# Two-layer trunk on one core: who multiplies the result's blocks by the last norm's weights

## The chip, the core and the metric

The kernel runs on one core of a Trainium2 chip. Its engines, as the profile names them: PE (TensorE, matrix products), DVE (VectorE), ACT (ScalarE), POOL (GpSimd) and SP (SyncE, which here only issues transfers). Each works through its own instructions in the order in which they stand in the program, and waits on semaphores for the others. The metric is the device time of one execution in microseconds; the median of several runs counts.

## The reference

With a depth of 1 the trunk has one layer, the attention, between two norms. The sequence has 256 rows, the model 4096 columns, 32 heads of 128:

```python
def rms_norm(x, g):
    xf = x.astype(jnp.float32)
    y = xf * lax.rsqrt(jnp.mean(xf * xf, axis=-1, keepdims=True) + RMS_EPS)
    return (y * g.astype(jnp.float32)).astype(x.dtype)

def attn_branch(xn, w_in, w_out):
    proj = xn @ w_in                               # 4096 x 16384
    q, k, v, g = jnp.split(proj, 4, axis=-1)
...
    o = stick_breaking_attention(to_heads(q), to_heads(k), to_heads(v))
...
    return (o * jax.nn.silu(g)) @ w_out            # 4096 x 4096

def reference(x, norm_attn, w_in_attn, w_out_attn, ..., final_norm):
    h = x + attn_branch(rms_norm(x, norm_attn), w_in_attn, w_out_attn)
    return rms_norm(h, final_norm)
```

All is float32. The change concerns the last line: `h` is divided by the root of its rows' mean square and multiplied by `final_norm`, one weight per column.

## The kernel before

**Units.** The two weight matrices are worked through in 20 units: 16 of `w_in` (the projections), then 4 of `w_out` (1024 columns of the result each, as two blocks `c` and `c + 1` of 512 columns, each for two halves `t` of the 256 rows). A unit has 16 steps `s` of 256 rows of the weights. In a "mixed" unit a step multiplies 2 x 2 blocks by a scheme with seven products instead of eight (a few steps use all eight); the combined weights of such a step are sums of blocks.

**What each engine does with a step.** SP loads the weights' tiles (`raw`). For a step with seven products GpSimd's queue issues two more transfers (`add_block`) that add a second weight block onto a `raw` tile in place; VectorE forms the other sums in `raw` (`sums`, three instructions). Each float32 operand is split into a high half (`wh`, by ScalarE's cast) and a low half (`wl`, by VectorE's subtraction `wl<-raw,wh`), and a product is three matmuls: high by high, high by low, low by high. TensorE adds them up in PSUM (`acc`). There are seven buffers for `raw`, seven for `wh`, five for `wl`, and four of a small ring "gh", which holds rows such as `xres` and `grow` below.

**The order.** No order is written out by hand. The class `Plan` (lines 113 to 245) simulates the engines while the program is written: each piece of work has an engine, an assumed cost in ns and a key (when it is due), and each engine takes the waiting piece with the smallest key when it becomes free. The order found in this way is the order in the program. `vector_ns(512)` is 600.

**The result's blocks.** When a `w_out` unit is done, `combine` builds the four blocks `h` of 128 x 512 from PSUM. During the next unit, at due places spread over its steps, `blocks_out` and `block_out` (lines 1052 to 1076) do the following for each of the four: load the weights of the norm for the block (`grow`, the same 512 values for all rows), load the rows of `x` (`xres`), add them to `h` on VectorE, take the squares' sum on ScalarE (`sq`), and then multiply `h` by `grow` in place (`gain_on`, line 1047), due 8 us behind the addition. This holds for six of the eight blocks, that is for 12 multiplications, four in each of the last three units. The last two blocks get their weights at the very end together with the rows' factor (`rows_out`). The other six are only scaled by that factor then, on VectorE or ScalarE, and stored.

**What the multiplication waits for and who waits for it.** It waits for `grow`, for the addition and for the square, which reads `h`. The buffer of `grow` is given back to the ring "gh" after the second of a block's two multiplications, and the next `grow` or `xres` load, on SP's queue, may be the one that gets it. In the attention's part `p<-spill` loads on GpSimd's queue use the same ring. The norm's final scaling of a block in `rows_out` reads what the multiplication wrote.

**GpSimd's work.** Apart from a few constants at the start it only issues transfers: `add_block`'s pairs, and the stores and loads of the attention's result (`spill`, `p`).

Of the kernel before, what the change touches and what calls it, by code (L numbers as in the profile page):

```python
# [14 lines left out]
ALU = mybir.AluOpType  # L15
# [13 lines left out]
W = 2 * CW  # L29
# [71 lines left out]
def vector_ns(n):  # L101
    return 67 + 1.0417 * n
# [146 lines left out]
def kernel(  # L249
# [10 lines left out]
    nc = Plan(tc)  # L260
# [65 lines left out]
    def soon(c=4.0):  # L326
        return nc.here + 1e3 * c


    def dve(emit, n, key=None, more=0, **kw):  # L330
        n = n if isinstance(n, tuple) else (n,)
        cost = sum(vector_ns(m) for m in n) + 122 * (len(n) - 1) + more
        return nc.work("vector", cost, emit, soon() if key is None else key, **kw)
# [280 lines left out]
    for k in range(WARM):  # L614
# [12 lines left out]
        out=tri_f, in_=tri_f, compare_op=ALU.is_ge, fill=0.0, base=0, pattern=[[-1, P]], channel_multiplier=1,  # L627
# [4 lines left out]
        out=off_f, in_=off_f, compare_op=ALU.is_ge, fill=0.0, base=0,  # L632
# [351 lines left out]
    hs, xres, grow = {}, {}, {}  # L984
# [62 lines left out]
    def gain_on(c, t, key=None):  # L1047
        h = hs[c, t]
        yield nc.until(("grow", c))
        yield dve(lambda: nc.vector.tensor_tensor(out=h, in0=h, in1=grow[c], op=ALU.mult), W, key)  # L1050

    def block_out(c, t, key):

        h = hs[c, t]
        yield nc.take("gh")
        yield load_out(c, t)
        yield nc.until(("xres", c, t))
        yield nc.take("att")
        yield dve(lambda: nc.vector.tensor_tensor(out=h, in0=h, in1=xres[c, t], op=ALU.add), W, key)
        nc.give("gh")  # L1060
        yield from squares(c, t, c, ALL, key)
        nc.give("att")
        yield from gain_on(c, t, key + GAIN_LATER * 1e3)
# [270 lines left out]
```

## Time and profile before

| what | value |
|---|---|
| median of 3 runs | 1699.45 us (1698.41 to 1699.9) |
| the profiled execution | 1698.9 us |
| its span, from the first to the last instruction | 1697.1 us |
| mean granted TensorE clock | 0.997 |
| instructions | 25128 |
| the multiplications `h<-h,grow` on VectorE | 12, from 1461.8 to 1669.9 us |

The page of a profile gives busy times by engine and, from the last instruction backwards, the chain of work that ended last. An instruction stands as engine, operation, written tile <- read tiles, shape; nearly all have line 132, that of a helper through which the engines are called, so they are told apart by their tiles. In the views of instructions in order of time, the first two numbers are the start and the duration in us (merged instructions have a count x2, x3), and a bracket at the end gives the engine's idle time just before and what ended it. In the groups of waits, the numbers are the total in us, how often, and the longest.

### The profile page before, as it was taken

The page shows a single profiled execution, that of the slowest core. Times are in us where ns is not written, and L with a number is a line of the kernel's source. Part 1 is how long each engine was busy: PE and PEld are TensorE (multiplying, and loading weights), DVE is VectorE, ACT ScalarE, POOL GpSimd, SP SyncE. Part 2 cuts the span into 40 slices and gives each one's busy share as a digit, 9 for nine tenths or more (in the row PEclk, how much of TensorE's full clock was granted, in tenths as well). Part 3 has the DMA queues.
Part 4 walks back from the last instruction along what each step waited for, and adds up shares of the span by engine and source line. Part 5 has one row for each costly group of instructions (what it writes and reads, how often), then busy time and mean ns, then how long its engine had stood idle before and what let it go on. Part 6 is the DMA issues. An engine that isn't in the chain of part 4 may idle for free.

```text
span 1697.1 us, 25128 instructions
## 1 busy us (share of the span) xinstructions
PE 1680.2 (99%) x7776; PEld 1417.4 (84%) x7776; DVE 1602.0 (94%) x2025; ACT 1206.7 (71%) x1665; POOL 324.9 (19%) x400
## 2 busy tenths in 40 slices
PE   9999999999999999999999999999999999999997
PEld 7888888888888888888888888888888888888885
DVE  8899999999999999999999999999999978999997
ACT  8986767676767676767676767676868775656654
POOL 0012222121222222222212121212122111212110
PEclk9999999999999999999999999999999999999998
DMA  9978888878787878797978797979797978888895
GB/s 343 332 197 247 232 247 222 252 217 253 215 256 212 256 212 266 199 272 196 276 201 269 198 268 196 272 198 269 204 264 210 300 230 266 245 245 256 246 304 185
DMA packets 248438, 412.77 MB, mean 243 GB/s; under 512 B 28016, under 2 KB 72560, under 8 KB 248304
## 3 DMA queue, kind: packets, MB, share of 16 engines
q1 hardware_dynamic: 194544, 354.24, 62.7%
q0 software_dynamic: 53472, 56.65, 20.0%
q8 instruction: 61, 1.00, 0.2%
q14 instruction: 73, 0.60, 0.1%
q10 hardware_dynamic: 288, 0.28, 0.1%
HBM read 402.93 MB, written 8.13 MB: 242 GB/s over the span
## 4 chain that ended last, share of the span: by engine, by line
PE 94%; DVE 3%; DMA 1%; issue 1%; ACT 1%; SPq 0%; DVEq 0%; ACTq 0%
PE acc L132 89%; PE z L132 3%; PE o L132 1%; DVE wl L132 1%; PE tr L132 1%; DVE h L132 1%; DVE raw L132 0%; ACT wh L132 0%; DMA raw<-in_w_out_dram 0%; DMA raw<-in_w_in_dram 0%; DMA xres<-in_x_dram 0%; SPq L132 0%; ACT sq L132 0%; DVE scalars L132 0%; DVE qk_sb L132 0%
## 5 line engine op out<-in xcount | busy, mean ns | idle before, releaser
L132 ACT CAST wh<-raw 128x1024 fp32r<-128x1024 f32 (+1 forms) x989 | 919.3, 970 | 385.5 <-DVE raw L132 160.9
L132 DVE TENSOR_TENSOR wl<-raw,wh 128x1024 fp32r<-128x1024 f32 (+1 forms) x815 | 975.7, 1220 | 49.3 <-ACT wh L132 23.9
L132 PE MATMUL acc<-wh,sh 128*128 128x512 f32 x2048 | 771.9, 389 | 0.1
L132 PE MATMUL acc<-wh,sl 128*128 128x512 f32 x1898 | 727.1, 383 | 1.8 <-DVE sl L132 1.8
L132 PE MATMUL acc<-wl,sh 128*128 128x512 f32 x1748 | 668.9, 383 | 0.1
L132 PEld LDWEIGHTS acc<-wh,sh 128*128 128x128 f32 x2048 | 384.0, 188 | 77.9 <-DVE qk_sb L132 4.9
L132 POOL DMA_DIRECT2D raw<-in_w_in_dram x300 | 258.3, 947 | 972.2 <-DMA raw<-in_w_in_dram 375.1
L132 PEld LDWEIGHTS acc<-wh,sl 128*128 128x128 f32 x1898 | 356.0, 188 | 66.3 <-DVE sl L132 2.4
L132 PEld LDWEIGHTS acc<-wl,sh 128*128 128x128 f32 x1748 | 328.4, 188 | 55.6 <-DVE wl L132 0.4
L132 DVE TENSOR_TENSOR raw<-raw,raw 128x512 f32<-128x512 f32 x348 | 238.3, 688 | 15.3 <-DMA raw<-in_w_in_dram 11.7
L132 PE MATMUL acc<-wh,oh 128*128 128x512 f32 x512 | 192.4, 383 | 0.0
L132 PE MATMUL acc<-wh,ol 128*128 128x512 f32 x488 | 186.7, 383 | 0.0
L132 PE MATMUL acc<-wl,oh 128*128 128x512 f32 x464 | 177.6, 383 | 1.4 <-DVE wl L132 1.4
L132 DVE TENSOR_TENSOR wh<-raw,wh 128x512 fp32r<-128x512 f32 x174 | 119.7, 688 | 3.3 <-ACT wh L132 2.7
L132 DVE TENSOR_TENSOR raw<-raw 128x512 f32<-128x512 f32 x174 | 119.4, 686 | 0.0
L132 PEld LDWEIGHTS acc<-wh,oh 128*128 128x128 f32 x512 | 96.1, 188 | 17.3
L132 PEld LDWEIGHTS acc<-wh,ol 128*128 128x128 f32 x488 | 91.5, 188 | 16.1
L132 PEld LDWEIGHTS acc<-wl,oh 128*128 128x128 f32 x464 | 87.1, 188 | 17.6 <-DVE wl L132 2.2
L132 POOL DMA_DIRECT2D raw<-in_w_out_dram x48 | 41.5, 984 | 173.8 <-DMA raw<-in_w_out_dram 85.2
L132 ACT ACTIVATE f<-f 128x384 f32<-128x384 f32 x96 | 50.5, 526 | 3.0
L132 POOL DMA_DIRECT2D p<-spill x27 | 17.0, 676 | 89.9 <-DVE ol L132 32.0
L132 DVE SCALAR_TENSOR_TENSOR gv_sb<-acc,scalars,gv_sb 128x512 f32<-128x512 f32 x45 | 33.5, 745 | 0.0
(86 smaller groups left out, 765.7 us busy)
## 6 DMA issues: line engine op xcount, KB each, us to landing
raw<-in_w_in_dram SPq DMA_DIRECT2D x1024, 256.0 KB, 4.5
raw<-in_w_out_dram SPq DMA_DIRECT2D x256, 256.0 KB, 4.5
raw<-in_w_in_dram POOLq DMA_DIRECT2D x300, 128.0 KB, 5.2
p<-spill POOLq DMA_DIRECT2D x27, 256.0 KB, 4.6
raw<-in_w_out_dram POOLq DMA_DIRECT2D x48, 128.0 KB, 5.4
xr<-in_x_dram SPq DMA_DIRECT2D x16, 256.0 KB, 5.3
xres<-in_x_dram SPq DMA_DIRECT2D x16, 256.0 KB, 5.5
out_dram<-h SPq DMA_DIRECT2D x16, 256.0 KB, 2.8
```

The costliest lines, as they stand in the source:

```text
L132: return self.tc.keep_in_program_order(getattr(self.engine, name)(*args, **kw))
```

## The change

The multiplication by the last norm's weights goes from VectorE's instruction stream to GpSimd's. The instruction and its operands stay the same; it stands in GpSimd's queue among the transfers that this engine issues. The planner's assumed cost is 1000 ns instead of VectorE's 600. The due time is unchanged.

```diff
     def gain_on(c, t, key=None):
         h = hs[c, t]
         yield nc.until(("grow", c))
-        yield dve(lambda: nc.vector.tensor_tensor(out=h, in0=h, in1=grow[c], op=ALU.mult), W, key)
+        yield nc.work(
+            "gpsimd", 1000, lambda: nc.gpsimd.tensor_tensor(out=h, in0=h, in1=grow[c], op=ALU.mult), key
+        )
 
     def block_out(c, t, key):
```

## The prediction

> **What bounds the kernel now.** I read the page's busy line and chain first, then the stages of the last three units, then the waits of TensorE, and last the order of instructions on VectorE around the multiplications.
>
> ```profile
> PE 1680.2 (99%) x7776; PEld 1417.4 (84%) x7776; DVE 1602.0 (94%) x2025; ACT 1206.7 (71%) x1665; POOL 324.9 (19%) x400
> PE 94%; DVE 3%; DMA 1%; issue 1%; ACT 1%; SPq 0%; DVEq 0%; ACTq 0%
> ```
>
> TensorE is never idle for long: 94% of the chain is its own work, and VectorE, at 94% busy, is the only other engine with a real share. So work taken off VectorE is worth only what TensorE waits for it. The stages from 1450 us on, which hold all twelve multiplications (the first at 1461.8, the last at 1669.9 us, both shown below), say how much that is; the columns are from:to, length, then busy time and instructions of each engine.
>
> ```profile
> core 0: us, PE busy (x) PEld busy (x) DVE busy (x) ACT busy (x) POOL busy (x), PEclk, DMA share, GB/s
> 1450.00:1500.00 50.00, 50.00 (x229) 42.55 (x228) 47.89 (x56) 32.74 (x41) 12.04 (x14) 1.00 0.94 280
> 1500.00:1550.00 50.00, 49.71 (x225) 41.78 (x224) 47.74 (x57) 28.91 (x34) 8.71 (x11) 1.00 0.84 247
> 1550.00:1600.00 50.00, 48.92 (x223) 41.35 (x222) 48.52 (x58) 32.05 (x43) 9.77 (x12) 1.00 0.88 259
> 1600.00:1650.00 50.00, 50.00 (x227) 42.22 (x226) 47.21 (x61) 29.73 (x39) 8.36 (x11) 1.00 0.92 285
> 1650.00:1680.00 30.00, 30.00 (x138) 25.54 (x137) 26.53 (x33) 16.64 (x23) 0.86 (x1) 1.00 0.54 164
> ```
>
> ```profile
> PE acc L132 <- DVE wl L132: 1.4, 2, 1.1
> 1515.60 0.50 PE L132 MATMUL acc<-wl,oh 128*128 128x512 f32 x1 [0.29 <-DVE wl L132]
> 1581.34 0.49 PE L132 MATMUL acc<-wl,oh 128*128 128x512 f32 x1 [1.08 <-DVE wl L132]
> ```
>
> In these 230 us TensorE waits twice, 1.4 us together, both times for a low half (wl) from VectorE: once at the end of the first of the three units, once near the end of the second, never in the third. VectorE is at its limit just ahead of both. That is all that a lighter VectorE could win, and it is also where a heavier VectorE is paid for at once.
>
> **The change part by part.** Removed: twelve multiplications on VectorE.
>
> ```profile
> L132 DVE TENSOR_TENSOR h<-h,grow 128x512 f32<-128x512 f32 x12 | 8.3, 688 | 0.0
> 1577.11 0.70 DVE L132 TENSOR_TENSOR raw<-raw,raw 128x512 f32<-128x512 f32 x1
> 1577.71 0.70 DVE L132 TENSOR_TENSOR h<-h,grow 128x512 f32<-128x512 f32 x1
> 1578.32 0.70 DVE L132 TENSOR_TENSOR raw<-raw 128x512 f32<-128x512 f32 x1
> ```
>
> One takes 0.69 us, but the next starts 0.60 us after it (1577.71 to 1578.32), the last 0.09 us being overlapped. So 12 x 0.60 = 7.2 us of VectorE's time go, four per unit.
>
> Added: the same twelve on GpSimd, which does no arithmetic there now. The only rows of its arithmetic are at the start:
>
> ```profile
> 0.31 0.10 POOL L1321 MEMSET const-float32-0.0<- 128x1 f32 x1 [0.31 <-issue]
> 4.56 0.20 POOL L132 MEMSET squares_f<- 128x128 f32 x1 [3.19 <-DVE idle L132]
> 4.83 0.29 POOL L132 TENSOR_SCALAR_AFFINE_SELECT squares_f<-squares_f 128x128 f32<-128x128 f32 x1
> 5.34 0.40 POOL L132 TENSOR_SCALAR_AFFINE_SELECT squares_f<-squares_f 128x128 f32<-128x128 f32 x1
> 5.24 0.35 DVE L132 TENSOR_SCALAR sh<-xs,gcol 128x256 fp32r<-128x256 f32 x1 [0.71 <-DMA xs<-in_xT_dram]
> 6.63 0.34 DVE L132 TENSOR_SCALAR sh<-xs,gcol 128x256 fp32r<-128x256 f32 x1
> ```
>
> A fixed 0.10 us; 128 columns written take 0.20, read and written 0.29, and the same instruction takes 0.40 where VectorE reads SBUF beside it (5.24 to 5.59). These rows are the one hint in this trace that the two engines disturb each other. Scaled to 512 columns: 0.5 us by the memset (0.10 + 4 x 0.10), 0.86 by the quiet select, 0.10 + 4 x 0.30 = 1.30 by the disturbed one, 2.5 if the second operand doubles the disturbed rate. I take 1.30, since VectorE is nearly always at work in these units.
>
> What it costs VectorE isn't shown. One end: nothing, and VectorE simply gains 0.60 each time. The other: VectorE stands still for the whole of each multiplication, because nearly everything it does there (wl<-raw,wh; raw<-raw,raw; h<-h,xres) reads two operands in SBUF, as GpSimd's new instruction does. I take the second, being nearest to the disturbed row. VectorE's work then finishes before GpSimd's begins, so the 0.09 us of overlap is lost as well: 1.30 + 0.09 - 0.60 = 0.79, or 0.8 us more per multiplication.
>
> The Trainium skill, "SBUF — State Buffer", section "SBUF: two separate sides", speaks against the change in the same way: VectorE and GpSimd share a pair of ports, given as an exclusive lock for a whole instruction to a VectorE instruction with two SBUF inputs or to a GpSimd instruction that reads SBUF, and the loser blocks fully. Its "GPSIMD Engine Reference", section "Elementwise — side-by-side cycle accounting", measures 4497 ns for 2048 columns of such an addition; a quarter, 1.12 us as an estimate, would make the 0.8 us 0.6. Only the run can show either.
>
> Now place by place, with VectorE's order and its idle time ahead of an instruction in brackets:
>
> ```profile
> 1461.78 0.68 DVE L132 TENSOR_TENSOR h<-h,grow 128x512 f32<-128x512 f32 x1
> 1469.36 1.23 DVE L132 TENSOR_TENSOR wl<-raw,wh 128x1024 fp32r<-128x1024 f32 x1 [0.35 <-issue]
> 1482.61 1.23 DVE L132 TENSOR_TENSOR wl<-raw,wh 128x1024 fp32r<-128x1024 f32 x1 [0.26 <-PE acc L132]
> 1519.68 0.69 DVE L132 TENSOR_TENSOR wh<-raw,wh 128x512 fp32r<-128x512 f32 x1 [1.26 <-ACT wh L132]
> 1543.12 0.68 DVE L132 TENSOR_TENSOR h<-h,grow 128x512 f32<-128x512 f32 x1
> 1556.67 3.50 DVE L132 TENSOR_TENSOR wl<-raw,wh 128x1024 fp32r<-128x1024 f32 x3 [0.63 <-ACT wh L132]
> 1519.03 0.62 ACT L132 CAST wh<-raw 128x512 fp32r<-128x512 f32 x1 [3.17 <-DMA raw<-in_w_out_dram]
> ```
>
> First unit: from its first multiplication at 1461.8 to TensorE's wait at 1515.6 VectorE is idle 0.35 + 0.26 = 0.61 us. Four times 0.8 is 3.2, less 0.61: TensorE waits 2.6 us more. Second unit: from 1543.1 to 1581.3 it is idle 0.63 us, so 3.2 - 0.63 = 2.6 more. Between the two VectorE can catch up some of the first delay in the 1.26 us at 1519.7, which a weight transfer ended and not TensorE: less 1.3. Third unit: TensorE never waits, and VectorE is idle 50.00 - 47.21 + 30.00 - 26.53 = 6.3 us, which covers 3.2; without that cover it would be 3.2. Sum: 2.6 + 2.6 - 1.3 = 3.9 us. At the ends: hold of 0.5 us, nothing; hold of 2.5 us, 2.0 more per multiplication, 8.0 - 0.6 + 8.0 - 0.6 - 1.3 = 13.5, and 8.0 - 6.3 = 1.7 of the third unit, 15 us.
>
> GpSimd's queue is the other place. It issues the adding transfers (raw, twice per quad), and each multiplication now stands between them, waiting for ScalarE's square and for the weights of the norm.
>
> ```profile
> raw<-in_w_out_dram POOLq DMA_DIRECT2D x48, 128.0 KB, 5.4
> 1573.08 1.73 POOL L132 DMA_DIRECT2D raw<-in_w_out_dram  x2 [6.69 <-DVE raw L132]
> 1585.20 1.43 DVE L132 TENSOR_TENSOR raw<-raw,raw 128x512 f32<-128x512 f32 x2
> ```
>
> The pair at 1573.1 lands by about 1573.1 + 0.9 + 5.4 = 1579.4 and is first used at 1585.2, 5.8 us later. A multiplication of 1.3 us ahead of it is hidden by that; a longer one, above 5.8 us, would not be. I cost it at nothing. The last norm's output is hidden too: the final scaling comes 12 us behind the last multiplication, and its extra wait, now for another engine, is long over.
>
> ```profile
> 1669.90 0.69 DVE L132 TENSOR_TENSOR h<-h,grow 128x512 f32<-128x512 f32 x1
> 1682.41 0.49 DVE L132 TENSOR_SCALAR h<-h,scalars 128x512 f32<-128x512 f32 x1
> ```
>
> The order that the planner writes is moved a little as well, since it now sees 600 ns less on VectorE and 1000 ns on a nearly empty engine; that can go either way by a fraction of an instruction, and I put it at nothing, with 1 us to both sides.
>
> The profiled execution took 1698.9 us (span 1697.1), 0.55 under the median of the runs. 1698.9 + 3.9 = 1702.8, and against the median 1703.4.
>
> **The rivals.** **A**, the forecast: VectorE stands still, +3.9 us, 1703.4.
>
> **B**, the other side: the engines work side by side, or GpSimd gets in between without holding VectorE. From a hold of under 0.51 us on, VectorE gains. Then up to 4 x 0.60 = 2.4 us per unit cover the 0.29 and the 1.08 us of waiting: 1.4 us, 1698.1. The counts of matmuls (225 and 223 beside 229) allow some 0.6 us more of small gaps: 1697.4. More isn't there to be had, since TensorE is fully busy otherwise. Against it: the 0.40 row; for it: that row is a single one, and VectorE's instruction beside it took 0.35, hardly more than its like a little later (0.34).
>
> **C**: the queue decides. A multiplication that the order puts behind an adding transfer waits for what this waits for, and the next loads of the small row buffers wait for it.
>
> ```profile
> 1551.12 0.19 ACT L132 ACTIVATION_READ_ACCUMULATOR sq<-h 128x1 f32 x1
> 1551.55 0.68 DVE L132 TENSOR_TENSOR h<-h,grow 128x512 f32<-128x512 f32 x1
> 1552.50 0.57 SPq L132 DMA_DIRECT2D grow<-in_gain_out_dram  x1
> 1553.40 0.33 SPq L132 DMA_DIRECT2D xres<-in_x_dram  x1
> 1555.82 1.73 POOL L132 DMA_DIRECT2D raw<-in_w_out_dram  x2 [6.77 <-DVE raw L132]
> 1560.81 0.68 DVE L132 TENSOR_TENSOR h<-h,xres 128x512 f32<-128x512 f32 x1
> xres<-in_x_dram SPq DMA_DIRECT2D x16, 256.0 KB, 5.5
> ```
>
> If the multiplication of 1551.6 came behind the pair of 1555.8, it would end at 1557.5 + 1.3 = 1558.8, 6.6 us later than now (1552.2). Grow and the xres behind it on SP would follow as they do now, xres 1.2 us after the multiplication's end (1553.4); so xres would be issued at 1560.0 and there at 1565.5, and VectorE, which now takes it at 1560.8, would stand for 4.7 us in the stretch that ends in TensorE's wait: 1704.2 alone, 1708.1 on top of A. For it: GpSimd's queue is in order and idles up to 7 us at such a wait. Against: ScalarE's square ends at 1551.3, when that queue is empty, so the planner should put the multiplication first.
>
> **How the numbers follow.** 0.2% (3.4 us) is about what a measurement of this kernel can tell from no change; the limits are 1696.1 and 1702.9. A 0.67, of which 0.52 above the upper limit (longer holds push up far more than shorter ones pull down) and 0.15 within. B 0.18: 0.04 below the lower limit, by luck in the order, and 0.14 within. C 0.15: 0.12 above, 0.01 within, and 0.02 for another order that helps, below. Faster 0.06, same 0.30, slower 0.64. The range goes from B's 1697.8 to 1711, which is A with a hold of about 2.2 us, or A and C with one at 1.7.
>
> **What would show it.** Right: GpSimd's group h<-h,grow x12 with a mean of 1.1 to 1.6 us; VectorE's instructions that start beside one stretched, or a gap of about that size ahead of them, ended by no producer; TensorE's waits for wl grown from 1.4 to about 5 us, around 1515 and 1581, and still none after 1600. B is right if VectorE's mean durations stay at 689 and 1223 ns and those two waits vanish. C is right if GpSimd's multiplications start several us after their squares end and VectorE waits for xres, or for raw from an adding transfer. The prediction is wrong in kind if TensorE's extra waits come in the third unit or in the tail after 1676.

## The result: slower, and more by a queue than by VectorE

| | before | changed |
|---|---|---|
| median | 1699.45 us | 1705.59 us |
| lowest to highest of 5 runs | 1698.41 to 1699.9 | 1704.25 to 1710.58 |
| the profiled execution | 1698.9 | 1705.43 |
| its span | 1697.1 | 1703.7 |

The ratio is 1.0046 (95% interval 1.0034 to 1.0057): slower by 6.1 us, where 3.9 were forecast. (The ratios here and below are not the quotients of the two medians, which here would be 1.0036.) The runs now lie 6 us apart, four times as wide as before.

The page and TensorE's waits of the changed kernel, as they were read before (a wait's numbers are the total in us, how often, and the longest; the lines with a time are single matmuls, with the wait ahead of them in brackets):

```profile
PE 1681.0 (99%) x7776; PEld 1415.7 (83%) x7776; DVE 1607.9 (94%) x2013; ACT 1205.3 (71%) x1665; POOL 373.6 (22%) x412
PE acc L132 <- DVE wl L132: 5.3, 4, 1.8
PE acc L132 <- DVE h L132: 2.6, 1, 2.6
```

```profile
1528.05 0.47 PE L132 MATMUL acc<-wh,oh 128*128 128x512 f32 x1 [2.56 <-DVE h L132]
1568.84 0.49 PE L132 MATMUL acc<-wl,oh 128*128 128x512 f32 x1 [1.33 <-DVE wl L132]
1584.60 0.52 PE L132 MATMUL acc<-wl,oh 128*128 128x512 f32 x1 [0.73 <-DVE wl L132]
1601.39 0.50 PE L132 MATMUL acc<-wl,oh 128*128 128x512 f32 x1 [1.83 <-DVE wl L132]
1681.33 0.48 PE L132 MATMUL acc<-wl,oh 128*128 128x512 f32 x1 [1.37 <-DVE wl L132]
```

TensorE now waits 7.8 us in these units where it waited 1.4: 6.4 us, which is nearly all of the 6.6 by which the span grew. VectorE has twelve instructions fewer (2013 beside 2025) and is busy 5.9 us longer. Its groups in these units show where, before and after (busy us, mean ns, then idle us):

```profile
L132 DVE TENSOR_TENSOR wl<-raw,wh 128x1024 fp32r<-128x1024 f32 x118 | 140.1, 1223 | 10.3 <-ACT wh L132 7.9 <-DMA raw<-in_w_out_dram 1.5 <-issue 0.4
L132 DVE TENSOR_TENSOR raw<-raw,raw 128x512 f32<-128x512 f32 x48 | 33.1, 689 | 1.3 <-DMA raw<-in_w_out_dram 0.8
```

```profile
L132 DVE TENSOR_TENSOR wl<-raw,wh 128x1024 fp32r<-128x1024 f32 x117 | 142.6, 1258 | 10.2 <-ACT wh L132 10.0
L132 DVE TENSOR_TENSOR raw<-raw,raw 128x512 f32<-128x512 f32 x48 | 38.9, 809 | 3.7 <-DMA raw<-in_w_out_dram 3.1
L132 DVE TENSOR_TENSOR raw<-raw 128x512 f32<-128x512 f32 x24 | 17.6, 732 | 0.0
```

The same instructions take longer: 117 x 35 ns + 48 x 120 ns + 24 x 44 ns (688 before) = 4.1 + 5.8 + 1.1 = 11.0 us for twelve multiplications, 0.9 us each, while 0.60 each was saved. Those are not a few per cent on every instruction but, on average, about 1 us on one instruction beside each multiplication. And two multiplications are of another kind altogether. The first line is GpSimd's group (min/median/max ns, first and last start); then come single instructions of GpSimd and VectorE in order of time, and last the issue of one pair of adding transfers in the kernel before:

```profile
L132 POOL TENSOR_TENSOR h<-h,grow x12: 1331/1436/18466, 1460.8 to 1674.1; 128x512 f32<-128x512 f32 x12
1469.93 1.38 POOL L132 TENSOR_TENSOR h<-h,grow 128x512 f32<-128x512 f32 x1 [2.08 <-ACT sq L132]
1501.35 18.47 POOL L132 TENSOR_TENSOR h<-h,grow 128x512 f32<-128x512 f32 x1 [0.73 <-ACT sq L132]
1519.76 3.53 POOL L132 DMA_DIRECT2D raw<-in_w_out_dram  x4
1578.33 11.97 POOL L132 TENSOR_TENSOR h<-h,grow 128x512 f32<-128x512 f32 x1
1590.25 1.76 POOL L132 DMA_DIRECT2D raw<-in_w_out_dram  x2
```

```profile
1468.94 3.44 DVE L132 TENSOR_TENSOR wl<-raw,wh 128x1024 fp32r<-128x1024 f32 x2
1518.57 2.01 DVE L132 TENSOR_TENSOR h<-acc,h 128x512 f32<-128x512 f32 x3
1525.40 0.69 DVE L132 TENSOR_TENSOR raw<-raw,raw 128x512 f32<-128x512 f32 x1 [3.09 <-DMA raw<-in_w_out_dram]
1588.47 0.69 DVE L132 TENSOR_TENSOR raw<-raw,raw 128x512 f32<-128x512 f32 x1
1589.19 1.66 DVE L132 TENSOR_TENSOR raw<-raw,raw 128x512 f32<-128x512 f32 x1
```

```profile
1511.55 1.73 POOL L132 DMA_DIRECT2D raw<-in_w_out_dram  x2 [11.49 <-DVE raw L132]
```

Two wl in a row take 2.36 us undisturbed; beside the multiplication of 1469.9 they take 3.44. The one of 1501.4 lasts 18.5 us: VectorE goes on without a break, and GpSimd ends 1.2 us after VectorE's first instruction that reads PSUM (h<-acc,h at 1518.6). Four adding transfers stood behind it in GpSimd's queue and are issued at 1519.8; before the change the first two of the four went out at 1511.6. VectorE waits 3.09 us for them, the additions h<-acc,h behind it in VectorE's order come late, and so TensorE gets a PSUM bank 2.56 us late, at 1528.

The second drawn-out multiplication, of 1578.3, ends at a break of another kind. VectorE's instruction of 1588.47 ends at 1589.16, and the next one starts only at 1589.19; GpSimd ends 1.1 us behind that, at 1590.3, and the instruction of 1589.19 takes 1.66 us instead of 0.69. VectorE does not wait for the transfers behind this one. Most of the ten short multiplications find such a break at once; two, at 1565.7 and 1674.1, get in without one.

### The profile page after: what moved, and what is told of

Read it like the earlier page. It is cut to its first block, busy times and chain, and to the rows that moved or that the text cites. A ratio compares the mean times of both kernels' runs of the same rounds, so it can differ in the third digit from the quotient of the medians.

```text
span 1703.7 us, 25137 instructions
## 1 busy us (share of the span) xinstructions
PE 1681.0 (99%) x7776; PEld 1415.7 (83%) x7776; DVE 1607.9 (94%) x2013; ACT 1205.3 (71%) x1665; POOL 373.6 (22%) x412
## 5 line engine op out<-in xcount | busy, mean ns | idle before, releaser
L132 POOL DMA_DIRECT2D raw<-in_w_in_dram x300 | 261.9, 966 | 970.6 <-DMA raw<-in_w_in_dram 316.2
L132 DVE TENSOR_TENSOR raw<-raw,raw 128x512 f32<-128x512 f32 x348 | 243.8, 704 | 14.9 <-DMA raw<-in_w_in_dram 8.8
L132 POOL TENSOR_TENSOR h<-h,grow 128x512 f32<-128x512 f32 x12 | 45.1, 3762 | 58.2 <-ACT sq L132 37.0
```

The costliest lines, as they stand in the source:

```text
L132: return self.tc.keep_in_program_order(getattr(self.engine, name)(*args, **kw))
```

## The experiments

Two questions: is it the planner's other order, the place in GpSimd's queue, or the reading of SBUF that costs? And how much is VectorE standing, how much the two drawn-out multiplications?

**The order alone, and nothing at all.** `e1_order` keeps the planning and issues the multiplication on VectorE; `e2_leftout` keeps the planning and leaves it out.

```diff
-            "gpsimd", 1000, lambda: nc.gpsimd.tensor_tensor(out=h, in0=h, in1=grow[c], op=ALU.mult), key
+            "gpsimd", 1000, lambda: nc.vector.tensor_tensor(out=h, in0=h, in1=grow[c], op=ALU.mult), key
```
```diff
+        yield nc.work("gpsimd", 1000, lambda: None, key)
```

> The changed kernel's planning (1000 ns on GpSimd's queue), but the multiplication is issued on VectorE. Exclusion theory: the order alone costs little, VectorE loses the 12 x 0.60 us again and there is no meeting with GpSimd: 1698.5 to 1701, TensorE waiting 1 to 3 us in the last three units. Theory that the planner's other order costs the time: 1704 to 1707, as the changed kernel. Theory of the queue (a multiplication in GpSimd's queue waits for the square and holds up the transfers): as before the change, 1699 to 1700.

> The changed kernel's planning, with the multiplication left out on every engine, so six of eight blocks of the output lack the last norm's weights. Exclusion theory: TensorE's waits in the last three units shrink below 1 us, 1697.4 to 1698.6; this is the most that any place for the multiplication can win. Theory of the order: 1703 to 1706, as the order is that of the changed kernel. Theory of the queue: 1697.4 to 1698.6 as well.

Measured beside 1699.08 for the kernel before: 1698.71 (ratio 0.9995, 0.9986 to 1.0004) and 1697.70 (0.9993, 0.9984 to 1.0002). The order costs nothing. Without any multiplication the median is 1.4 us lower. That is as much as TensorE's waits in the profile of before, but the interval doesn't exclude nothing, and the profile of `e2_leftout` still has one wait for wl, of 1.0 us, at 1595.6. So the size agrees; that just these waits went is not shown.

**The queue without the reading.** `e3_memset` has a memset in the same place, waiting for the same square.

```diff
+        yield nc.work("gpsimd", 1000, lambda: nc.gpsimd.memset(h, 1.0), key)
```

> The changed kernel with a memset of the same block on GpSimd in place of the multiplication (those blocks of the output are constants): the same place in the queue, the same wait for the square, but nothing is read from SBUF. Exclusion theory: GpSimd's memsets take 0.5 to 0.7 us all twelve, none is drawn out, VectorE's instructions keep 0.69 and 1.22 us, and the time is that of the kernel with the multiplication left out, 1697.4 to 1699. Theory of the queue: 1703 to 1706, since it waits for the square as the multiplication does. Theory of the order: 1703 to 1706.

Measured: 1697.45 (0.9989, 0.9980 to 0.9998). GpSimd's group:

```profile
L132 POOL MEMSET h<- x12: 524/526/858, 1461.7 to 1666.8; 128x512 f32 x12
```

None is drawn out, and VectorE keeps its 689 and 1222 ns. So with so short an instruction neither a place in the queue nor the wait for the square costs anything. What is left as the cause is that GpSimd reads SBUF while VectorE does, or that it is longer than a memset; the trials below part the two.

**The two engines by themselves.** `e6_ports` sets one instruction of GpSimd beside streams of VectorE, all instructions of a stream writing one buffer; in `e7_stream` each writes its own (the cut is from the second).

```python
def trial(stream, work, reads_e=True):
    tt(dve, e, g, k)               # reads what GpSimd wrote in the trial before
    stream[0](0)
    dve.tensor_scalar(out=e, in0=a, ...)   # GpSimd may start behind this
...
    work()                         # two_in: tt(pool, g, e, k)
    for i, f in enumerate(stream[1:], 1):
        f(i)                       # both: a * b, bank: PSUM * b, single: a * 2
```

> Nothing of the trunk is computed: the kernel holds eleven trials, in each of which GpSimd gets one instruction of 128x512 while VectorE runs some 18 instructions of one kind back to back (and two trials in which GpSimd runs first). Theory 1 (exclusion: an instruction of VectorE with two operands in SBUF and one of GpSimd that reads SBUF never run together, and GpSimd is passed over as long as VectorE goes on without a break): beside two-operand instructions GpSimd's multiplication lasts about the rest of the stream, 18 x 0.60 = 11 us (12 instructions of 1024 columns: 10 x 1.14 = 11 us); with one instruction that reads PSUM in the middle it gets in there, after about 8 x 0.60 = 5 us, and VectorE then stands for 1 to 1.4 us; beside a stream that reads PSUM and one SBUF operand it lasts as long as alone, 1.0 to 1.4 us; a memset, which reads nothing, lasts as long as alone in any stream. Where GpSimd runs first, VectorE's two-operand instruction begins only when GpSimd's is over. Theory 2 (the two only slow one another): 1.5 to 3 us in all streams, VectorE's instructions each some per cent longer, no waiting until the stream ends. Theory 3 (no disturbance; the long ones in the kernel waited for something else): as long as alone in all.

> Nothing of the trunk is computed: trials as in e6_ports, but every instruction of VectorE's streams writes a buffer of its own, so that they overlap (a pitch of 0.60 us at a duration of 0.69) and leave no gap, as in the trunk. Theory of the gap (GpSimd gets in only where VectorE's next instruction starts behind the end of the last, or where it reads PSUM or a single operand): beside 19 two-operand instructions GpSimd's multiplication lasts about as long as the stream, 10 to 12 us, and VectorE's stream isn't lengthened; with one instruction at the middle that reads PSUM, or one that reads a single operand, or one that reads the result of its predecessor, it ends about 6 to 8 us after its start, and VectorE stands for about 1 us there; beside the streams that read PSUM 1.3 us; a memset 0.52 us. Rival (it gets in at the next end of an instruction whatever the pitch): 1.3 to 2.1 us in all trials, as in e6_ports.

First `e6_ports`: GpSimd alone, beside two operands in SBUF, beside PSUM and SBUF, and a memset; then VectorE's streams of 18 beside the second and the fourth:

```profile
7.17 1.26 POOL L18 TENSOR_TENSOR g<-e,k 128x512 f32<-128x512 f32 x1 [6.74 <-DVE e L18]
10.97 1.58 POOL L18 TENSOR_TENSOR g<-e,k 128x512 f32<-128x512 f32 x1 [2.53 <-DVE e L18]
27.12 1.26 POOL L18 TENSOR_TENSOR g<-e,k 128x512 f32<-128x512 f32 x1 [14.57 <-DVE e L18]
119.17 0.52 POOL L18 MEMSET g<- 128x512 f32 x1 [13.95 <-DVE g L18]
```

```profile
10.74 13.98 DVE L18 TENSOR_TENSOR o<-a,b 128x512 f32<-128x512 f32 x18
119.03 13.04 DVE L18 TENSOR_TENSOR o<-a,b 128x512 f32<-128x512 f32 x18
```

The multiplication takes 1.26 us alone, and the same beside a stream that reads PSUM. Beside two SBUF operands VectorE's stream is 13.98 - 13.04 = 0.94 us longer than beside the memset: that is the price of one meeting. But GpSimd was not passed over, as theory 1 had expected: 1.58 us instead of 11. The pitch says why that trial was no copy of the trunk: 13.04 / 18 = 0.72 us, since each instruction waited for the last one's write, against 0.60 in the trunk. There is a small gap behind each. `e7_stream` takes it away; in this order, GpSimd beside PSUM and SBUF, beside 19 of one operand, beside two operands with one reading PSUM in the middle, the same with one of a single operand in the middle, the same with one in the middle that reads its predecessor's result, and a one-operand instruction of GpSimd beside two operands; then VectorE's instruction that reads PSUM in the third of these, and its streams of 19 beside a multiplication that got in at once and beside a memset:

```profile
21.69 1.27 POOL L18 TENSOR_TENSOR g<-e,k 128x512 f32<-128x512 f32 x1 [12.46 <-DVE e L18]
34.32 7.35 POOL L18 TENSOR_TENSOR g<-e,k 128x512 f32<-128x512 f32 x1 [11.36 <-DVE e L18]
56.84 6.39 POOL L18 TENSOR_TENSOR g<-e,k 128x512 f32<-128x512 f32 x1 [10.72 <-DVE e L18]
70.28 12.14 POOL L18 TENSOR_TENSOR g<-e,k 128x512 f32<-128x512 f32 x1 [7.05 <-DVE e L18]
84.24 1.57 POOL L18 TENSOR_TENSOR g<-e,k 128x512 f32<-128x512 f32 x1 [1.81 <-DVE e L18]
98.43 12.62 POOL L18 TENSOR_SCALAR g<-e 128x512 f32<-128x512 f32 x1 [12.62 <-DVE e L18]
```

```profile
62.02 0.69 DVE L18 TENSOR_TENSOR o<-c,b 128x512 f32<-128x512 f32 x1
7.42 12.59 DVE L18 TENSOR_TENSOR o<-a,b 128x512 f32<-128x512 f32 x19
112.97 11.52 DVE L18 TENSOR_TENSOR o<-a,b 128x512 f32<-128x512 f32 x19
```

Now GpSimd is passed over: to the end of the stream (12.14 and 12.62, and 7.35 beside the short one-operand instructions), or to the instruction that reads PSUM: 56.84 + 6.39 = 63.23 is 1.2 us, a multiplication's length, behind 62.02. In the one trial of it, a single instruction that scales one operand from SBUF is no opening, against what was expected. In three of the trials with a gapless stream it got in at once instead (1.6 us beside two operands, 2.1 beside those of 1024 columns, and the 1.57 above, long before the instruction that was to let it in). Up to the middle the trials of 56.84 and 84.24 are the same program. So without a gap it looks like chance whether GpSimd gets in at the first instruction's end or has to wait for an opening; nothing that was read in these profiles tells the two cases apart. Where it got in at once, VectorE's stream is 12.59 - 11.52 = 1.07 us longer, nearly the price of before.

**Ten or two.** `e4_ten` puts the two drawn-out multiplications on VectorE and leaves ten on GpSimd, `e5_two` does the reverse ("not in" in the diff's first line), `e11_two_again` is `e5_two` once more.

```diff
+        if (c, t) in ((1, 1), (3, 1)):
+            yield dve(lambda: nc.vector.tensor_tensor(out=h, in0=h, in1=grow[c], op=ALU.mult), W, key)
+        else:
             yield nc.work(
                 "gpsimd", 1000, lambda: nc.gpsimd.tensor_tensor(out=h, in0=h, in1=grow[c], op=ALU.mult), key
```

> Ten multiplications on GpSimd, and the two that were drawn out (the second half of the second block, in the first and in the second of the three units) on VectorE. Theory that most of the loss comes from the two drawn-out ones, which hold up the adding transfers behind them: 1700 to 1702, with no multiplication above 2.5 us (if the planner's new order doesn't draw out another). Theory that most comes from VectorE standing for about 1 us at each of the ten others: 1703 to 1705.

> The reverse: only those two on GpSimd, the ten others on VectorE. Theory of the drawn-out ones: 1702 to 1705, both again above 8 us and TensorE waiting over 2 us behind each. Theory of the ten: 1699 to 1701.

Measured beside 1699.07: ten 1700.94 (ratio 1.0012, 1.0003 to 1.0020), two 1705.75 (1.0032, 1.0019 to 1.0046; runs from 1699.13 to 1710.29), a little above the 1702 to 1705 expected. Two of the twelve cost what all twelve cost, ten cost 1.9 us. They don't add up. In the profile of `e5_two` (an execution of 1709.82), GpSimd's two multiplications, and behind the second of them VectorE and TensorE:

```profile
1502.35 19.14 POOL L132 TENSOR_TENSOR h<-h,grow 128x512 f32<-128x512 f32 x1
1578.55 10.77 POOL L132 TENSOR_TENSOR h<-h,grow 128x512 f32<-128x512 f32 x1 [8.32 <-ACT sq L132]
1595.08 0.69 DVE L132 TENSOR_TENSOR raw<-raw,raw 128x512 f32<-128x512 f32 x1 [6.91 <-DMA raw<-in_w_out_dram]
1598.23 0.50 PE L132 MATMUL acc<-wh,oh 128*128 128x512 f32 x1 [3.28 <-ACT wh L132]
```

Here VectorE also waits for the transfers behind the second one, 6.9 us, which it does not in the changed kernel. That fits a VectorE that waits less for late transfers where the ten have made it late, but no run tried it.

**Openings.** `e10_two_let_in` is `e5_two` with three short copies out of PSUM on VectorE behind the place of each of the two; `e9_let_in` is the changed kernel with them behind all twelve.

```diff
+    def let_in(bank):
...
+        for _ in range(3):
+            yield nc.work(
+                "vector", 130, lambda: nc.vector.tensor_copy(few[0], bank[:, 0:64]), nc.here - 1e5, wait=1300
+            )
```

> e5_two (only the two multiplications that are drawn out are on GpSimd) with the same three short instructions behind each of the two. Theory of the gap: both under 5 us, 1699 to 1701, and the runs lie within 2 us of one another. Rival: 1705 to 1707 with a spread of 10 us, as e5_two.

> e5_two unchanged, beside the one with openings on the same chip: again 1699 to 1711 with a wide spread, the median near 1705, if it is by chance whether GpSimd gets in at once. If the spread was the chip's: within 2 us.

> The changed kernel, with three short instructions of VectorE (64 columns copied out of PSUM) behind each multiplication's place, about 1.4 us apart in the plan: openings for GpSimd, at a cost of about 36 x 0.1 to 0.15 us of VectorE's time. Theory of the gap (a multiplication is drawn out because VectorE's overlapping two-operand instructions leave no opening, and what it costs is the adding transfers behind it): no multiplication above some 5 us, TensorE's wait of 2.6 us near 1528 gone, 1700.5 to 1703.5, under the changed kernel's 1705.6 in spite of the 36 added instructions. Rival (the drawn-out ones are long for another reason, or what they hold up doesn't matter): 1706 to 1709, since VectorE only gets more to do.

On one chip, beside 1698.85: with openings 1698.56 (ratio 1.0000, 0.9991 to 1.0008), without 1707.19 (1.0041, 1.0027 to 1.0054; 1700.04 to 1707.9). The first is just under the expected 1699, and its runs, from 1697.99 to 1701.0, lie 3 us apart and not within 2. Its two multiplications, the first of its copies that opened the way, and VectorE's sums in both kernels, first with and then without:

```profile
1499.42 2.96 POOL L132 TENSOR_TENSOR h<-h,grow 128x512 f32<-128x512 f32 x1
1580.18 2.81 POOL L132 TENSOR_TENSOR h<-h,grow 128x512 f32<-128x512 f32 x1 [7.55 <-PE acc L132]
1501.16 0.21 DVE L132 COPY few<-sq 128x64 f32<-128x64 f32 x1
L132 DVE TENSOR_TENSOR raw<-raw,raw 128x512 f32<-128x512 f32 x48 | 32.9, 686 | 0.5
```

```profile
L132 DVE TENSOR_TENSOR raw<-raw,raw 128x512 f32<-128x512 f32 x48 | 33.0, 688 | 11.1 <-DMA raw<-in_w_out_dram 10.6
```

From 19.1 and 10.8 us to 3.0 and 2.8 by six instructions of 0.2 us: the first multiplication ends 1.2 us behind the start of a copy, the same 1.2 us as behind 62.02 in the trial. VectorE's 10.6 us of waiting for the adding transfers are gone, and the time is 8.6 us shorter. That settles the second mechanism.

With openings at all twelve the time is 1704.97 (1.0037, 1.0025 to 1.0049), above the expected 1700.5 to 1703.5:

```profile
L132 POOL TENSOR_TENSOR h<-h,grow x12: 1317/1800/3242, 1461.8 to 1673.8; 128x512 f32<-128x512 f32 x12
L132 DVE COPY few<-sq x36: 209/216/219, 1464.7 to 1681.0; 128x64 f32<-128x64 f32 x36
PE acc L132 <- DVE wl L132: 6.6, 7, 2.0
```

No multiplication is above 3.3 us and no wait for PSUM is left, but TensorE waits 6.6 us for wl: 36 copies of 0.22 us, up to 7.8 us, are more than VectorE has to spare, on top of the twelve meetings. Openings at all twelve are no remedy.

**Another place on VectorE.** `e8_late` leaves all twelve on VectorE but does the first eight in the third unit, where it has idle time; their weights are loaded there.

```diff
+    def late_gains():
+        for c in range(4):
+            yield nc.until(("used", LAST, step_at(LAST, 5 + 2 * c)))
+            yield nc.take("gh")
+            yield load_gain(c)
+            for t in range(NT):
+                yield from gain_on(c, t, place_at(LAST, 7 + 2 * c + t))
+            nc.give("gh")
```

> From the kernel before: all twelve on VectorE, but the eight of the first two of the three units are done in the third, where VectorE has 6 us of idle time (their weights are loaded there). If VectorE's load in the first two units is what TensorE's 1.4 us of waiting there come from, and the third has the room: 1697.6 to 1698.6. If the third has no room for 8 x 0.60 = 4.8 us more: 1699 to 1702.

Measured: 1707.97 (1.0055, 1.0043 to 1.0067), a miss. VectorE's view near the end, and the stores, before and here:

```profile
1682.93 10.21 SPq L132 DMA_DIRECT2D out_dram<-h  x16
```

```profile
1679.63 0.69 DVE L132 TENSOR_TENSOR h<-h,xres 128x512 f32<-128x512 f32 x1 [3.54 <-DMA xres<-in_x_dram]
1683.45 1.29 DVE L132 TENSOR_TENSOR h<-h,grow 128x512 f32<-128x512 f32 x2 [1.59 <-DMA grow<-in_gain_out_dram]
1694.66 9.97 SPq L132 DMA_DIRECT2D out_dram<-h  x16
PE acc L132 <- DVE wl L132: 0.6, 1, 0.6
```

TensorE's waits do shrink, to 0.6 us, but the loads of the added weights share the four row buffers with xres, of which two hold a result block in the third unit; xres comes late, the last blocks' work is pushed behind TensorE's end, and the stores begin 11.7 us later (in a profiled execution of 1710.45, the longest of its runs). VectorE's idle time was there, the buffers weren't.

## Why the prediction held, and where it was off

**What bounds the kernel**: right. TensorE's own waits account for 6.4 of the 6.6 us. The leave-out and the memset are 1.4 and 1.6 us under the kernel before (only the second is clear of noise), about the 1.4 to 2.0 us that were called the most to be won.

**The price of a multiplication for VectorE** was right in kind and too high: 1.39 us of standing were taken, about 0.95 are measured (0.94 and 1.07 in the trials, 0.9 over the twelve), so 0.3 to 0.4 us net and not 0.8. GpSimd's instruction itself, taken at 1.30, is 1.26 alone and 1.33 to 1.7 us in the kernel, but VectorE is held for less than its length. The ten that are only of this kind cost 1.9 us. The estimate from the Trainium skill, "GPSIMD Engine Reference", section "Elementwise — side-by-side cycle accounting", was 1.12 us, a little below the measured 1.26. The Trainium skill, "SBUF — State Buffer", section "SBUF: two separate sides", has this exclusion, and says under "Who interferes with whom" that an instruction of VectorE with at most one operand in SBUF, outside certain faster modes, does not contend with GpSimd. The trials agree (1.27 us beside PSUM and one SBUF operand, 0.94 us of standing beside two).

**The step that failed** is the one on GpSimd's queue: "A multiplication of 1.3 us ahead of it is hidden by that; a longer one, above 5.8 us, would not be. I cost it at nothing." Two were longer, 18.5 and 12.0 us, because the exclusion also works the other way: GpSimd can be kept waiting for as long as VectorE's instructions overlap. That is the larger part of the loss: with these two back on VectorE (`e4_ten`) 4.2 of the 6.1 us are gone. The changed kernel's own profile traces only the 2.56 us at 1528 to it; how the 5.3 us of waiting for wl divide between the two mechanisms stays open. It was in reach: the quoted rows of before show a pitch of 0.60 at a duration of 0.69, which leaves no opening. The forecast asked only what GpSimd does to VectorE. So 3.9 us forecast and 6.1 measured are nearer than the working deserves: one term was twice too large, another was missing.

**The places**: the second unit's waits came (1568.8, 1584.6, 1601.4) and the first unit's as well, but as a late PSUM bank at 1528. "Still none after 1600" is wrong: 1.83 us at 1601.4 and 1.37 at 1681.3, so 3.2 of the 7.8 us. By the prediction's own last sign, extra waits in the third unit or after 1676, it is wrong in kind there. The 6.3 us of idle time that were to cover the third unit's multiplications did not lie where they were needed. Ahead of 1681.3 VectorE has none from 1673.1 on:

```profile
1673.10 5.72 DVE L132 TENSOR_TENSOR wl<-raw,wh 128x1024 fp32r<-128x1024 f32 x4
```

Four wl in a row take about 4.6 us undisturbed (4 x 1.22, less three overlaps of 0.09); the 1.1 us more stand beside the multiplication of 1674.1. That points to this meeting for the last wait, but no run tried it, and for the wait at 1601.4 the cause stays open.

**The rivals.** B (side by side, 1697.4 to 1698.1) falls: that is what a memset does, 1697.45. C named the right place, the queue, and one of its signs came, VectorE's wait for an adding transfer. Its way into the queue was wrong: no multiplication waited long behind a transfer, and VectorE never waited for xres. That GpSimd's wait for the square costs nothing is shown by the memset.

## What to carry to other kernels

Before elementwise work is moved to GpSimd, look at what VectorE does at that time: if its instructions have two operands in SBUF, a meeting cost VectorE here about three quarters of the length of GpSimd's instruction (0.94 of 1.26 us), and a VectorE without gaps can keep GpSimd waiting for many microseconds. A stream that scales one operand from SBUF kept it waiting as well (7.35 us). Then ask what stands behind the moved instruction in GpSimd's queue, here the adding transfers, and how late these may be. An engine that is idle for 81% of the time is no free place if its instructions and those of the one that is to be relieved hold each other up.

## What was not expected of the hardware

Whether GpSimd gets in looks partly like chance: in one kernel the same start of a trial gave 1.57 and 6.39 us. The same program also ran 1699.1 and 1710.3 us (`e5_two`, and again 1700.0 and 1707.9 in `e11_two_again`), but only executions of 1709.8 and 1707.7 were profiled, so it is an inference that the multiplications got in at once in the short ones. VectorE's wait of a few hundredths of a microsecond for its own last write (a pitch of 0.72 us instead of 0.60) was enough of an opening in the trials of `e6_ports`, and so is an instruction that reads 64 columns of PSUM; an instruction that scales one operand from SBUF was not. GpSimd's one-operand multiplication by a constant took 1.49 us alone, longer than the 1.26 of the two-operand one (`e6_ports`).
